# A hybrid decoder block on one core: the branch gates as seven products of halves, kept in DRAM until the projections

## The chip, the cores and the metric

The kernel runs on one core of one Trainium2 chip. The metric is the device time of one execution in microseconds; of several runs the median is given. PE is TensorE's matmul stream, PEld its weight loads, DVE is VectorE, ACT ScalarE, POOL GpSimd, SP the engine whose queue issues most DMAs.

## What is computed

One layer (D_MODEL 1024, SEQ 1024, all float32): an input projection whose columns feed four causal mixers and four gates, the gated sum of the mixers' outputs, an output projection, and a squared-ReLU MLP. The part around the change:

```python
h = rms_norm(x, norm_mix_g[l]) * (1.0 + sc1) + sh1
p = h @ w_in[l]
y_a = rwkv7_mixer(p[..., :OFF_B], ...)          # ends in ... @ rwkv_out
y_b = spatial_gating_mixer(p[..., OFF_B:OFF_C], ...)   # ... @ sg_out
y_c = short_conv_mixer(p[..., OFF_C:OFF_D], ...)       # ... @ conv_out
y_d = s5_mixer(p[..., OFF_D:OFF_G], ...)        # h = gelu(y) @ glu_w; h[:1024] * sigmoid(h[1024:])
gates = jax.nn.sigmoid(p[..., OFF_G:]).reshape(bsz, seq, N_BRANCH, D_MODEL)
merged = (gates[:, :, 0] * y_a + gates[:, :, 1] * y_b
          + gates[:, :, 2] * y_c + gates[:, :, 3] * y_d)
x = x + gt1 * (merged @ w_o[l])
```

## The kernel before, in words

Every matmul of float32 operands is three matmuls of a rounded and a remainder part: an operand is split into `hi` (ScalarE, a cast, L72) and `lo` (VectorE, the source minus `hi`, L73), and `mm3` (L110) issues hi·hi, hi·lo and lo·hi into one PSUM bank. The normed input stands in SBUF as `hh[k]`, `hl[k]`: 8 tiles of 128 features by 1024 tokens. Weights come block by block through a queue of loads (`weight_queue`, L1699; `take`, L101): a DMA on SP's queue into `raw`, then the split into `whi`, `wlo`, two buffers each.

A gate block is 128 of the 4 × 1024 gate columns. `h_mm` (L777) computes it for one half of the tokens with 8 × 3 matmuls of 128x512. `gates` (L1200) goes branch by branch (3, 1, 2 and, last, 0), block by block, half by half: gate product, sigmoid on ScalarE (L1222), the branch's own projection (6 matmuls, 12 for branch 3, whose output is a GLU), the product of the two on VectorE (L1236) and the sum over branches on POOL (L1239) or, for branch 0, on VectorE (L1241). A branch's mixer output waits in DRAM (`MX`).

Beside this runs a background: `step` (L119), called after each `mm3` (a beat), advances generators whose `yield n` asks to be called n beats later. In the stretch of the gates the background is the RWKV mixer: `rwkv_1` (L927, eight units; four feature rows are mixed, decayed and stored), `rwkv_2` (the inverse of triangular 32x32 blocks, 31 steps of a multiplication, L1051, and a sum, L1053, on VectorE) and `rwkv_3` (eight units of small matmuls, a chain in time). `mods` (L289) sums 64 slices of a weight matrix on VectorE (`macc`, L310 and L312) for later modulation vectors. Branch 0 needs the RWKV mixer, so its gates come last. Then `w_o` (L1252) and the MLP follow; the MLP's two products already use seven products of halves in place of eight.

A scheduler orders the instructions of each engine when the program is built; each engine then runs its list in order.

Of the kernel before, what the change touches and what calls it, by code (L numbers as in the profile page):

```python
# [16 lines left out]
P = 128  # L17
# [23 lines left out]
class Kern:  # L41
# [247 lines left out]
    def mods(self, M):  # L289
# [16 lines left out]
        acc = M.tile([P, HALF], F32, tag="acc", name="macc")  # L306
        for i, (sec, hf, kt) in enumerate(parts):
            w = ws[i]
            if kt == 0:
                v.tensor_scalar(acc, w, self.cact[:, 0:1], None, op0=ALU.mult)  # L310
            else:
                v.scalar_tensor_tensor(acc, w, self.cact[:, kt : kt + 1], acc, op0=ALU.mult, op1=ALU.add)  # L312
# [3 lines left out]
            if kt < KT - 1:  # L316
                continue
            pt = self.ps()
            if sec in (3, 4):
                for j in range(4):  # L320
                    self.mm(pt[:, j : j + 1], acc[:, j * P : j * P + P], self.ones)
                c = slice(4 * hf, 4 * hf + 4)
                dst = (self.sh2, self.s2)[sec - 3]
                v.tensor_tensor(dst[:, c], pt[:, :4], self.cols("ada_b")[:, sec * 8 + 4 * hf : sec * 8 + 4 * hf + 4], op=ALU.add)
                if sec == 4:
                    v.scalar_tensor_tensor(self.s2[:, c], self.s2[:, c], 1.0, self.cols("nfg")[:, c], op0=ALU.add, op1=ALU.mult)
            else:
# [872 lines left out]
    def gates(self, br, first, last):  # L1200
# [4 lines left out]
        if not first:  # L1205
            self.flush()
# [697 lines left out]
```

## Time and profile before

| | us |
|---|---|
| median of 3 runs (lowest, highest) | 1683.56 (1683.49, 1686.27) |
| the profiled execution's own time | 1685.38 |
| its span, first to last instruction | 1683.6 |
| PE busy, share of the span | 1612.0, 96% |
| mean granted TensorE clock | 0.991 |

The span is the time between the first and the last instruction; what lies around it is 1.8 us. Busy times are unions, so pipelined instructions of one engine that overlap are counted once. The stages follow each other in the span: to 353 us the norm, the first columns and the convolution; 353 to 824 the gates and projections of branches 3, 1, 2; 824 to 934 those of branch 0; 934 to 1056 the output projection and the second norm; then the MLP.

### The profile page before, as it was taken

The numbers are of one execution on the slowest core, as the hardware profiler recorded it, in microseconds if no ns is written. First come the engines' busy times: TensorE is split into PE (matmuls) and PEld (weight loads), VectorE is DVE, ScalarE is ACT, GpSimd is POOL, SyncE is SP. The second block draws the span as 40 slices with busy tenths as digits, with TensorE's granted clock in tenths as the row PEclk, the third lists the DMA queues.
The fourth block names the chain that finished last, engine by engine and source line by source line (L and its number), as shares of the span: only waits on it lengthen the run. The fifth ranks groups of instructions, "written<-read, shape, count | busy, mean of one in ns | idle before, by whom it ended". The sixth has DMA issues, their size and how long they took to land.

```text
span 1683.6 us, 22649 instructions
## 1 busy us (share of the span) xinstructions
PE 1612.0 (96%) x8083; PEld 1292.1 (77%) x8083; DVE 998.7 (59%) x1749; ACT 651.2 (39%) x1206; POOL 600.4 (36%) x485
## 2 busy tenths in 40 slices
PE   3999999999999999999999999999999999999996
PEld 2798778777777777777788877688888878888875
DVE  5673545766638824332433476965555478669986
ACT  4522134446522112212222244654554455444343
POOL 2260223112221213222101362186566465128662
PEclk9999999999999999999999999999999999999998
DMA  8423145777685245431211546364444584563332
GB/s 278 132 64 54 58 125 186 176 191 178 149 160 172 60 131 165 138 108 46 75 47 39 169 137 201 91 204 158 160 139 144 172 309 157 171 216 88 102 124 100
DMA packets 262723, 234.67 MB, mean 139 GB/s; under 512 B 79352, under 2 KB 194283, under 8 KB 262611
## 3 DMA queue, kind: packets, MB, share of 16 engines
q1 hardware_dynamic: 254002, 224.83, 44.5%
q10 hardware_dynamic: 8464, 8.01, 1.8%
q8 instruction: 64, 1.05, 0.3%
q0 software_dynamic: 144, 0.39, 0.1%
q14 instruction: 49, 0.39, 0.1%
HBM read 172.59 MB, written 60.58 MB: 138 GB/s over the span
## 4 chain that ended last, share of the span: by engine, by line
PE 36%; DVE 9%; DMA 2%; issue 2%; POOL 1%; ACT 1%; POOLq 0%; DVEq 0%; ACTq 0%; SPq 0%
PE pmm L112 21%; PE pax L112 8%; PE pch L112 7%; DVE g L73 3%; DVE xx L73 1%; DMA raw<-in_ffn_w_dram 1%; DVE m L1541 1%; DMA raw<-FA 1%; DVE n L73 1%; ACT g L72 0%; DVE wlo L73 0%; POOL ev L1531 0%; DVE m L1544 0%; DMA raw<-in_w_o_dram 0%; DVE xx L1439 0%
## 5 line engine op out<-in xcount | busy, mean ns | idle before, releaser
L112 PE MATMUL pmm<-hh,whi 128*128 128x512 f32 x704 | 285.2, 407 | 4.1 <-ACT hh L410 4.1
L112 PE MATMUL pmm<-hl,whi 128*128 128x512 f32 x704 | 278.7, 396 | 5.3 <-POOL hl L412 4.1
L112 PE MATMUL pmm<-hh,wlo 128*128 128x512 f32 x704 | 278.3, 395 | 0.0
L73 DVE TENSOR_TENSOR wlo<-raw,whi 128x512 fp32r<-128x512 f32 (+1 forms) x140 | 104.9, 786 | 130.8 <-ACT whi L72 127.6
L112 PEld LDWEIGHTS pmm<-hh,whi 128*128 128x128 f32 x704 | 132.6, 189 | 35.0 <-ACT hh L410 5.3
L112 PEld LDWEIGHTS pmm<-hl,whi 128*128 128x128 f32 x704 | 133.2, 189 | 33.7 <-POOL hl L412 4.5
L112 PEld LDWEIGHTS pmm<-hh,wlo 128*128 128x128 f32 x704 | 133.2, 189 | 29.6 <-issue 0.9
L72 ACT CAST whi<-raw 128x512 fp32r<-128x512 f32 (+1 forms) x140 | 79.0, 612 | 157.0 <-PE pmm L112 135.1
L112 PE MATMUL pmm<-g,g 128*128 128x512 f32 x456 | 107.3, 390 | 1.1 <-DVE xx L1439 1.1
L112 PE MATMUL pmm<-n,wyh 128*128 128x512 f32 x320 | 106.3, 411 | 0.8 <-ACT n L72 0.8
L73 DVE TENSOR_TENSOR g<-raw,g 128x512 fp32r<-128x512 f32 x75 | 72.0, 960 | 48.2 <-ACT g L72 48.1
L112 PEld LDWEIGHTS pmm<-g,g 128*128 128x128 f32 x456 | 85.6, 188 | 19.4 <-DVE xx L1439 1.5
L1222 ACT ACTIVATE sig<-pmm 128x512 f32<-128x512 f32 x64 | 38.2, 596 | 142.6 <-PE pmm L112 135.0
L1239 POOL TENSOR_TENSOR m<-m,sig 128x512 f32<-128x512 f32 x32 | 45.1, 1408 | 130.0 <-DVE sig L1236 129.8
L84 POOL TENSOR_TENSOR raw<-raw,gt 128x1024 f32<-128x1024 f32 x16 | 39.6, 2477 | 135.4 <-DMA raw<-in_w_o_dram 125.8
L112 PE MATMUL pmm<-g,m 128*128 128x512 f32 x256 | 81.4, 396 | 0.8 <-DVE g L73 0.6
L1236 DVE TENSOR_TENSOR sig<-pmm,sig 128x512 f32<-128x512 f32 x48 | 33.0, 686 | 69.1 <-PE pmm L112 69.0
L72 ACT CAST g<-raw 128x512 fp32r<-128x512 f32 x75 | 46.5, 620 | 69.4 <-PE pmm L112 34.5
L112 PEld LDWEIGHTS pmm<-n,wyh 128*128 128x128 f32 x320 | 60.4, 193 | 16.4 <-issue 1.2
L112 PE MATMUL pch<-g,g 128*128 128x512 f32 x222 | 59.5, 402 | 8.5 <-DVE g L73 5.7
L73 DVE TENSOR_TENSOR g<-w,g 128x512 fp32r<-128x512 f32 x65 | 64.9, 999 | 4.1 <-ACT g L72 4.1
L112 PE MATMUL pmm<-n,wyl 128*128 128x512 f32 x160 | 64.5, 403 | 0.0
(487 smaller groups left out, 3760.6 us busy)
## 6 DMA issues: line engine op xcount, KB each, us to landing
raw<-FA SPq DMA_DIRECT2D x56, 512.0 KB
raw<-in_w_in_dram SPq DMA_DIRECT2D x52, 512.0 KB
FA<-xx SPq DMA_DIRECT2D x80, 256.0 KB
raw<-in_ffn_w_dram SPq DMA_DIRECT2D x36, 512.0 KB
mod<-in_ada_w_dram SPq DMA_DIRECT2D x64, 256.0 KB
w<-in_ffn_w_dram SPq DMA_DIRECT2D x32, 512.0 KB
raw<-in_w_o_dram SPq DMA_DIRECT2D x16, 512.0 KB
FA<-ev SPq DMA_DIRECT2D x32, 256.0 KB
```

What stands on the lines that cost most here:

```text
L72: a = nc.scalar.copy(hi, src)
L73: b = (eng or nc.vector).tensor_tensor(lo, src, hi.bitcast(F32), op=ALU.subtract)
L84: nc.gpsimd.tensor_tensor(raw, raw, scale, op=ALU.mult)
L112: mm = lambda *x, **y: self.nc.tensor.matmul(*x, **y, skip_group_check=open_)
L1222: nc.scalar.activation(sg, pg, AF.Sigmoid)
L1236: v.tensor_tensor(m if first else sg, py[0], sg, op=ALU.mult)
L1239: nc.gpsimd.tensor_tensor(m, m, sg, op=ALU.add)
L1541: v.tensor_tensor(dst, x, y, op=ALU.add)
```

## The change

All gates come first. `gate_queue` and `gates` take the blocks in 16 pairs (256 gate columns), cut features, columns and tokens in halves and form each pair in seven products of 12 matmuls (Winograd's form), in an order written out by hand that weaves two pairs. The sums of halves of `h` (`h_sums`, during the convolution, and `h_blocks`) and of the weights are made on VectorE, as is one addition for three of a pair's four results; a bank accumulates products 1, 6, 7, 4 (another 5, 3) and is read in between. Weight halves are loaded on ACT's queue. The sigmoids go to a new DRAM tensor `G` (64 stores of 256 KB) and are read back (64 loads).

`merge` then does the projections: branches 3, 2, 1 woven block by block, `mx_load` having brought the mixer outputs into the tiles of `h`; then branch 0, between whose blocks the first three quarters of the output projection's first pass are placed (`next(out)`). `mods` defers a sum's matmul and its eviction by some beats (`mods_out`), and three `yield`s of `rwkv_1` grow (6 to 8, 6 to 10, 2 to 4). Cut to its core:

```diff
-                self.mm(pt[0:1], self.ones, acc)
-                yield 8
+            if kt == 2:
+                next(done, None)
+            elif kt == 4:
+                next(done, None)
+            elif kt == KT - 1:
+                done = self.mods_out(M, sec, hf, acc)
...
+    def h_sums(self):
+        for k in range(4):
+                v.tensor_tensor(f12, f(self.hh[k][:, c1]), f(self.hl[k][:, c1]), op=ALU.add)
+                v.tensor_tensor(f22, f(self.hh[k + 4][:, c1]), f(self.hl[k + 4][:, c1]), op=ALU.add)
+                v.tensor_tensor(t1, f12, f(self.hh[k][:, c0]), op=ALU.subtract)
+                v.tensor_tensor(t1, t1, f(self.hl[k][:, c0]), op=ALU.subtract)
...
+    def h_blocks(self):
+        for k in range(4):
+            self.split(self.hh[k][:, c1], self.hl[k][:, c1], self.t1[k])
+        for k in range(4):
+            v.tensor_tensor(self.f12[k], self.f22[k], self.f12[k], op=ALU.subtract)
+            v.tensor_tensor(self.f22[k], self.f22[k], self.t1[k], op=ALU.subtract)
...
+    def gate_queue(self):
+                seq += [(a, 2), (a - 1, 7)] if a > 2 else [(a - 1, 7), (a, 2)]
+                seq += [(a, 1), (a, 5), (a - 1, 4), (a, 6), (b, 2), (b, 1)]
+                seq += [(a, 7), (a, 3), (b, 5), (a, 4), (b, 6), (b, 3)]
...
+                nc.scalar.dma_start(raws[i, c], w[:, 4 * c : 4 * c + 4])
...
+            if k == 1:
+                v.tensor_tensor(A(1, 1), A(1, 1), A(2, 1), op=ALU.subtract)
+                v.tensor_tensor(A(2, 1), A(2, 1), A(2, 2), op=ALU.add)
+            elif k == 5:
+                v.tensor_tensor(A(2, 1), A(2, 2), A(1, 1), op=ALU.subtract)
+                v.tensor_tensor(A(1, 2), A(1, 2), A(2, 1), op=ALU.subtract)
...
+    def gates(self):
+        def out(i, r, c, t, src=None):
+            nc.scalar.activation(t, t if src is None else src, AF.Sigmoid)
+            self.store(self.G[br, j + r - 1, c - 1], t, 7)
+        for i, k in self.gate_seq:
+            hi, lo = self.take()
+            pt = banks[i % 2 + (2 if k in (2, 5, 3) else 0)]
+            for q in range(4):
+                self.mm3(pt, hi[:, q], lo[:, q], *B[k][q], q == 0 and k in (1, 5, 2), q == 3 and k in (4, 3, 2), open_=True)
...
+    def merge(self, todo, out=None):
+        for i, (br, j) in enumerate(todo):
+            wyh, wyl = self.take()
...
+            g_load(i + 3)
+            if (br, j) in ((0, 2), (0, 4), (0, 6)):
+                next(out)
...
+            self.conv(lambda r: r and next(sums, None))
+            self.depth = 3
+            self.h_blocks()
+            self.gates()
+            self.depth = 2
+            self.mx_load(1)
+            self.merge(self.blocks)
...
-            self.gates(0, False, True)
+            self.mx_load(0)
+            out = self.w_o()
+            self.merge([(0, j) for j in range(8)], out)
```

How the lists of the engines move, at the three places that matter below. TensorE, in the gates: before, the last two of the eight steps of a half block, and the projection behind them.

```order
L112 MATMUL pmm_3357<-hh_2_130,whi_2842 128x512
L112 MATMUL pmm_3357<-hl_2_138,whi_2842 128x512
L112 MATMUL pmm_3357<-hh_2_130,wlo_2843 128x512
L112 MATMUL pmm_3357<-hh_2_131,whi_2842 128x512
L112 MATMUL pmm_3357<-hl_2_139,whi_2842 128x512
L112 MATMUL pmm_3357<-hh_2_131,wlo_2843 128x512
L112 MATMUL pmm_3443<-n_3237,wyh_2851 128x512
L112 MATMUL pmm_3443<-n_3238,wyh_2851 128x512
L112 MATMUL pmm_3443<-n_3237,wyl_2852 128x512
```

Now, one product (`gh`, `gl`: the weight side's two parts, with the product's number 0 to 111; `m`: a made block of `h`). Four steps of three matmuls and no projection behind; a background matmul stands between.

```order
L103 MATMUL pmm_3190<-m_3129,gh_9_3432 128x512
L103 MATMUL pmm_3190<-m_3130,gh_9_3432 128x512
L103 MATMUL pmm_3190<-m_3129,gl_9_3433 128x512
L103 MATMUL pmm_3190<-m_3133,gh_9_3432 128x512
L103 MATMUL pmm_3190<-m_3134,gh_9_3432 128x512
L103 MATMUL pmm_3190<-m_3133,gl_9_3433 128x512
L133 MATMUL pax_3563<-ones,macc_3056 128x1 x4
L103 MATMUL pmm_3190<-m_3137,gh_9_3432 128x512
L103 MATMUL pmm_3190<-m_3138,gh_9_3432 128x512
L103 MATMUL pmm_3190<-m_3137,gl_9_3433 128x512
L103 MATMUL pmm_3190<-m_3141,gh_9_3432 128x512
L103 MATMUL pmm_3190<-m_3142,gh_9_3432 128x512
```

A block of 128 columns takes 48 matmuls before (two halves of 24), a pair of blocks 84 now.

VectorE, beside the triangular inverse (L1051 and L1053 before, L1056 and L1058 now): before, the remainder of a weight block (`wlo`), of a projection's weights (`wyl`) and the gate's product (L1236) stand between the steps.

```order
L73 TENSOR_TENSOR wlo_4895<-raw_4892,whi_4894 128x512 x2
L73 TENSOR_TENSOR wyl_4903<-wyr_4900,wyh_4902 128x256
L1051 TENSOR_TENSOR rpr_4497<-rti_4377,rta_4376 128x484
L1236 TENSOR_TENSOR sig_4941<-pmm_4943,sig_4941 128x512
L1053 TENSOR_REDUCE rti_4377<-rpr_4497 128x22
L312 SCALAR_TENSOR_TENSOR macc<-mod_4931,cact,macc 128x512
L1051 TENSOR_TENSOR rpr_4497<-rti_4377,rta_4376 128x529
L1236 TENSOR_TENSOR sig_4987<-pmm_4989,sig_4987 128x512
L1053 TENSOR_REDUCE rti_4377<-rpr_4497 128x23
```

Now a product's remainder (`gl`), the weight sums (L1267, L1268) and the additions from PSUM (L1308).

```order
L73 TENSOR_TENSOR gl_70_5427<-raw_5277,gh_70_5426 128x512
L1058 TENSOR_REDUCE rti_4880<-rpr_4998 128x25
L1267 TENSOR_TENSOR raw_5277<-raw_5277 128x4x128
L1308 TENSOR_TENSOR gp_5298<-pmm_3192,gp_5298 128x512
L1268 TENSOR_TENSOR raw_5277<-raw_5277,whi_5340 128x4x128
L1056 TENSOR_TENSOR rpr_4998<-rti_4880,rta_4879 128x676
L73 TENSOR_TENSOR gl_71_5448<-raw_5277,gh_71_5447 128x512
L1058 TENSOR_REDUCE rti_4880<-rpr_4998 128x26
L1270 TENSOR_TENSOR raw_5277<-whi_5340,raw_5277 128x4x128
L73 TENSOR_TENSOR gl_72_5470<-whi_5192,gh_72_5469 128x512
```

In seven products (84 matmuls) stand 14 instructions of the gates on VectorE: 7 remainders, 4 sums of weights, 3 additions. Before, a half block (30 matmuls with its projection) brought 2 or 3.

TensorE, at the end of the mixers: before, the output projection (`whi`, `wlo` against the merged `m`) follows the last gate block.

```order
L112 MATMUL pmm_8191<-hh_2_131,whi_7960 128x512
L112 MATMUL pmm_8191<-hl_2_139,whi_7960 128x512
L112 MATMUL pmm_8191<-hh_2_131,wlo_7961 128x512
L112 MATMUL pmm_8218<-n_7473,wyh_7969 128x512
L112 MATMUL pmm_8218<-n_7474,wyh_7969 128x512
L112 MATMUL pmm_8218<-n_7473,wyl_7970 128x512
L112 MATMUL pmm_8218<-n_7479,wyh_7969 128x512
L112 MATMUL pmm_8218<-n_7480,wyh_7969 128x512
L112 MATMUL pmm_8218<-n_7479,wyl_7970 128x512
L112 MATMUL pmm_8253<-whi_8056,m_7534 128x512
L112 MATMUL pmm_8253<-wlo_8057,m_7534 128x512
```

Now it begins in other banks (`pax`, `pch`) behind the first three projections of branch 0 (`mx` against `wyh`, `wyl`), with five still to come.

```order
L103 MATMUL pmm_8469<-mx_8361,wyh_8323 128x512 x2
L103 MATMUL pmm_8469<-mx_8361,wyl_8324 128x512
L103 MATMUL pmm_8482<-mx_8366,wyh_8323 128x512 x2
L103 MATMUL pmm_8482<-mx_8366,wyl_8324 128x512
L103 MATMUL pmm_8482<-mx_8371,wyh_8323 128x512 x2
L103 MATMUL pmm_8482<-mx_8371,wyl_8324 128x512
L103 MATMUL pax_8500<-whi_8389,m_8404 128x512
L103 MATMUL pax_8500<-wlo_8390,m_8404 128x512
L103 MATMUL pax_8500<-whi_8389,g_1273_8405 128x512
L103 MATMUL pax_8501<-whi_8389,m_8404 128x512
```

What stood between two projections, 24 matmuls of a gate, stands there no more.

## Rows read from the trace of the kernel before

**Rows 1.** Busy time of the whole execution, engine by engine, from the first part of the page (us, share of the span, instructions).

```profile
PE 1612.0 (96%) x8083; PEld 1292.1 (77%) x8083; DVE 998.7 (59%) x1749; ACT 651.2 (39%) x1206; POOL 600.4 (36%) x485
```

**Rows 2.** Busy time by stretch: the columns are the stretch and its length, then PE, PEld, DVE, ACT and POOL busy (us, and instructions started), the granted TensorE clock, the DMA share and GB/s. The five stretches are: gates beside the first RWKV stage; gates beside the triangular inverse (second stage); gates beside the third stage; the last branch's gates; the output projection.

```profile
353.00:471.00 118.00, 112.14 (x546) 87.38 (x545) 71.83 (x135) 69.97 (x117) 26.44 (x28) 0.97 0.70 170
514.80:580.40 65.60, 61.67 (x257) 48.29 (x256) 64.57 (x106) 14.94 (x29) 10.99 (x7) 0.97 0.45 137
621.00:810.00 189.00, 187.66 (x1563) 137.70 (x1560) 69.09 (x218) 40.93 (x100) 50.53 (x58) 1.00 0.35 103
825.00:934.00 109.00, 109.00 (x477) 89.18 (x476) 44.31 (x69) 29.05 (x54) 8.36 (x4) 1.00 0.18 55
934.00:1056.00 122.00, 116.14 (x524) 92.45 (x523) 78.82 (x122) 49.75 (x99) 52.60 (x31) 1.00 0.54 167
```

**Rows 3.** Who PE waited for between 340 and 600 us (us in total, times, longest us).

```profile
PE pax L142 <- DVE macc L312: 3.9, 2, 2.9
PE pch L142 <- DVE rar L981: 2.1, 2, 1.2
PE pch L142 <- DVE rt L937: 1.7, 1, 1.7
PE pch L142 <- DVE rbk L982: 1.0, 2, 0.9
PE pch L142 <- DVE ram L997: 0.8, 2, 0.6
PE pmm L112 <- ACT n L72: 0.8, 1, 0.8
```

**Rows 4.** Busy time by slices of 42 us, columns as in Rows 2: the three slices of the gates whose granted clock is under 1.00, and the slice with the most DMA traffic.

```profile
336.00:378.00 42.00, 38.14 (x190) 29.77 (x189) 29.39 (x60) 20.28 (x38) 6.63 (x7) 0.96 0.75 193
420.00:462.00 42.00, 40.54 (x186) 31.25 (x185) 24.76 (x47) 23.06 (x42) 9.10 (x11) 0.96 0.64 150
504.00:546.00 42.00, 39.10 (x162) 30.89 (x161) 33.72 (x74) 11.13 (x21) 5.46 (x4) 0.96 0.55 167
1344.00:1386.00 42.00, 40.29 (x173) 31.86 (x171) 28.55 (x30) 18.36 (x34) 25.77 (x17) 1.00 0.81 303
```

**Rows 5.** The same view for the instructions of L112 alone on PE (the wide matmuls), beside the first and the third RWKV stage.

```profile
353.00:471.00 118.00, 86.42 (x336) 0.97 0.70 170
621.00:810.00 189.00, 141.80 (x537) 1.00 0.35 103
```

**Rows 6.** Groups of instructions on DVE, shapes kept apart: line, engine, operation, out<-in, shape, count | busy us, mean ns of one | idle before, and what ended it.

```profile
L73 DVE TENSOR_TENSOR wlo<-raw,whi 128x512 fp32r<-128x512 f32 x132 | 99.8, 794 | 129.8 <-ACT whi L72 126.5 <-PE pmm L112 3.1
L73 DVE TENSOR_TENSOR xx<-w,xx 128x512 fp32r<-128x512 f32 x31 | 35.3, 1140 | 0.0
L1236 DVE TENSOR_TENSOR sig<-pmm,sig 128x512 f32<-128x512 f32 x48 | 33.0, 686 | 69.1 <-PE pmm L112 69.0
L73 DVE TENSOR_TENSOR wyl<-wyr,wyh 128x256 fp32r<-128x256 f32 x24 | 10.0, 415 | 0.1
L73 DVE TENSOR_TENSOR wyl<-wyr,wyh 128x512 fp32r<-128x512 f32 x8 | 5.5, 687 | 3.8 <-ACT wyh L72 3.8
L73 DVE TENSOR_TENSOR g<-sig,m 128x512 fp32r<-128x512 f32 x16 | 11.1, 692 | 11.0 <-ACT m L72 11.0
```

**Rows 7.** The multiplications (L1051) and the sums (L1053) of the triangular inverse alone, busy time in their stretch, one answer after the other (us, DVE busy with the count, granted clock, DMA share, GB/s).

```profile
514.80:580.40 65.60, 25.26 (x31) 0.97 0.45 137
514.80:580.40 65.60, 15.39 (x31) 0.97 0.45 137
```

**Rows 8.** DVE instructions in order of time in the last stage, while POOL is busy (start us, us, line, operation).

```profile
1512.40 1.28 DVE L1541 TENSOR_TENSOR m<-pmm,m 128x512 f32<-128x512 f32 x2
1513.60 0.68 DVE L73 TENSOR_TENSOR g<-w,g 128x512 fp32r<-128x512 f32 x1
1514.20 0.68 DVE L73 TENSOR_TENSOR g<-raw,g 128x512 fp32r<-128x512 f32 x1
1514.80 1.78 DVE L73 TENSOR_TENSOR g<-w,g 128x512 fp32r<-128x512 f32 x1
```

**Rows 9.** DVE, the last instruction of a unit of the first RWKV stage: the first unit's and the eighth's (start us, us).

```profile
303.70 0.41 DVE L1020 TENSOR_TENSOR rt<-pch,rt 128x256 f32<-128x256 f32 x1
471.01 0.41 DVE L1020 TENSOR_TENSOR rt<-pch,rt 128x256 f32<-128x256 f32 x1
```

**Rows 10.** Groups on ACT, columns as in Rows 6.

```profile
L72 ACT CAST whi<-raw 128x512 fp32r<-128x512 f32 x132 | 75.2, 618 | 153.1 <-PE pmm L112 135.1 <-DMA s_tt<-KP 10.3 <-PE pch L112 6.8
L1222 ACT ACTIVATE sig<-pmm 128x512 f32<-128x512 f32 x64 | 38.2, 596 | 142.6 <-PE pmm L112 135.0 <-POOL m L1239 7.5
L1623 ACT COPY m<-pmm 128x512 f32<-128x512 f32 x12 | 6.9, 586 | 8.2 <-PE pmm L112 7.9
L72 ACT CAST n<-ev 128x512 fp32r<-128x512 f32 x16 | 9.6, 616 | 6.9 <-DMA ev<-MX 6.3 <-PE pmm L112 0.6
```

**Rows 11.** A DMA issue on ACT's queue, in order of time (start us, us).

```profile
809.72 0.33 ACTq L1856 DMA_DIRECT2D gt<-GT  x1
```

**Rows 12.** Groups on POOL, columns as in Rows 6.

```profile
L84 POOL TENSOR_TENSOR raw<-raw,gt 128x1024 f32<-128x1024 f32 x16 | 39.6, 2477 | 135.4 <-DMA raw<-in_w_o_dram 125.8 <-DVE wlo L73 7.6 <-ACT hh L468 2.0
```

More of the change, by code (lines that the diff above doesn't have):

```diff
@@ L305, in mods @@
         yield 8
-        acc = M.tile([P, HALF], F32, tag="acc", name="macc")
+        done = iter(())
         for i, (sec, hf, kt) in enumerate(parts):
@@ new lines, in mods, with mods_out @@
+        yield 8
+        for _ in done:
+            yield 8
+    def mods_out(self, M, sec, hf, acc):
+        nc, v = self.nc, self.nc.vector
+        pt = self.ps()
+        if sec in (3, 4):
+            for j in range(4):
+                self.mm(pt[:, j : j + 1], acc[:, j * P : j * P + P], self.ones)
+            c = slice(4 * hf, 4 * hf + 4)
+            dst = (self.sh2, self.s2)[sec - 3]
+            v.tensor_tensor(dst[:, c], pt[:, :4], self.cols("ada_b")[:, sec * 8 + 4 * hf : sec * 8 + 4 * hf + 4], op=ALU.add)
+            if sec == 4:
+                v.scalar_tensor_tensor(self.s2[:, c], self.s2[:, c], 1.0, self.cols("nfg")[:, c], op0=ALU.add, op1=ALU.mult)
+        else:
+            self.n += 1
+            b = M.tile([1, HALF], F32, tag="w", name=f"mod_{self.n}", bufs=3)
+            c0 = sec * D + hf * HALF
+            nc.sync.dma_start(b, self.a["ada_b"][0:1, c0 : c0 + HALF])
+            self.mm(pt[0:1], self.ones, acc)
+            yield
+            v.tensor_tensor(b, pt[0:1], b, op=ALU.add)
+            nc.sync.dma_start(self.GT[sec // 4][0:1, hf * HALF : hf * HALF + HALF], b)
@@ L853, in sgu, with conv @@
             yield
-    def conv(self):
+    def conv(self, between):
         nc, v = self.nc, self.nc.vector
@@ L863, in conv @@
                 pt = self.h_mm(w, hf)
+                between(r)
                 cg.append(self.g(tag="n"))
@@ L1194, in wy_load, with mx_load @@
                 nc.sync.dma_start(wy[:, :, e], wsrc[:, :, e, cc])
[L1195 to L1196 removed]
+        hi = self.W.tile([P, 2, ne, P], F32R, tag="whi", name=f"wyh_{self.n}")
+        lo = self.W.tile([P, 2, ne, P], F32R, tag="wlo", name=f"wyl_{self.n}")
         self.split(hi, lo, wy)
[L1198 to L1207 removed]
+        return hi, lo
+    def mx_load(self, br):
+        self.flush()
+        self.mx[br] = [[None] * 2 for _ in range(2)]
+        tags = [("hh" if br in (3, 1) else "hl") + str(4 * (br in (1, 0)) + k) for k in range(4)]
         for hf in range(2):
@@ L1279, in w_o @@
                             self.store(self.X1[th * 4 + t, ch], x1[t][ch])
+                    if pc < 3 and not (th or ch):
+                        yield
             yield self.norm2(x1, xn, st, th)
@@ L1863, in build @@
             self.t2, self.t3, self.t4 = [], [], []
-            for bg in self.w_o():
+            for bg in out:
                 if self.bg is not None:
```

216 lines of the change are left out of this document (139 added, 77 removed).

## The prediction

> **What bounds the kernel now.** I read the busy times first: TensorE is busy 1612.0 of 1683.6 us, VectorE 998.7, ScalarE 651.2, POOL 600.4 [rows 1]. Then the same by stretch [rows 2]: in the last branch's gates TensorE is busy for all of 109.00 us, in which 477 matmuls start, so one wide matmul is worth 0.2285 us and each one removed is time removed, as long as the other engines keep up. Third, who TensorE waits for in the gates: VectorE, 10.3 us in all, 3.9 of it for the `mods` sums [rows 3]; three slices there have a granted clock of 0.96 [rows 4], which is half speed (1.2 of 2.4 GHz) for 0.04 x 42 / 0.5 = 3.4 us, or 1.7 us lost, after a wait each. So the reader should ask of the change: how many matmuls go, and which engine behind TensorE then has no room.
>
> **Matmuls removed.** The gates of 32 blocks take 32 x 48 = 1536 matmuls now, 16 pairs x 7 x 12 = 1344 after. Their shape is the same, so 192 x 0.2285 = **-43.9 us**. Projections, background and the rest issue the same matmuls as before.
>
> **Waits removed.** The `mods` sums are multiplied three slices late in place of at once: 3.9 us [rows 3] and the half-speed piece behind it [rows 4], 1.7, go: **-5.6**. The waits of the first RWKV stage (2.1 + 1.7 + 1.0 + 0.8) have longer yields now, but a fuller VectorE; I leave them as they are (bounds: 5.6 less; more is counted in the next step).
>
> **VectorE beside the first RWKV stage.** By the order of the lists, products 0 to 41 (504 matmuls, 115.2 us) go with six RWKV units. A unit takes (471.01 - 303.70) / 7 = 23.9 us before [rows 9]. The stretch of 118.00 us [rows 2] thus holds 4.9 units, and 336 wide matmuls [rows 5], 4.7 gate blocks. Less 336 x 0.2285 = 76.8 and 5.8 of waits, 35.4 us of small matmuls remain, 7.2 a unit. So TensorE needs 115.2 + 6 x 7.2 = 158 us. VectorE is busy 71.83 there; a gate block of branch 3 has 2 x 0.794 + 0.687 + 2 x 0.686 = 3.65 of it [rows 6], 17.0 in all, which leaves 54.8 of background, 67 for six units. A pair adds 7 remainders, 4 sums and 3 additions; two 128x512 operations on end take 1.28 us [rows 8], so 14 x 0.64 = 9.0, and 54 for six pairs. The blocks of `h` add 16 sums and differences behind the convolution and 16 remainders (the first 16 sums lie in the convolution): 32 x 0.64 = 20.5. In all 141 of 158 us: VectorE stays behind TensorE, at 90% in place of 61%. ScalarE: 69.97 less 4.7 x (3 x 0.618 + 4 x 0.596) [rows 2, 10] is 50, 61 for six units; a pair adds 7 x 0.618 + 3 x 0.586 + 4 x 0.596 and two loads at 0.33 [rows 10, 11], 9.1; 116 of 158. It too has room, but its loads stand in its list and wait until VectorE is done with the old half. At 90% with bursts at the start I take **+6** of new waits. Bounds: nothing, since the load fits; and 20, if each unit waits 3 us more, thrice what it waits now.
>
> **VectorE beside the inverse.** Its 31 steps take 25.26 + 15.39 = 40.7 us of VectorE [rows 7] and stand, by the lists, between the remainders of products 60 to 79: 20 x 12 x 0.2285 = 54.8 us of TensorE, with 20/7 x 9.0 = 25.7 for the products. 66.4 against 54.8: here VectorE is late by 11.6 us. Remainders are made three products ahead (depth 3), 8.2 us. So 3.4 us reach TensorE, with a half-speed piece of 1.7: **+5**. Bounds: 0 (now VectorE is busy 64.57 of 65.60 there [rows 2] and TensorE waits for the `mods` sums alone) and 13 (no lead).
>
> **From gates to projections.** The tiles into which `G` is read back are read by the last pair's product 7 till its end, so the first reads land only behind it; two groups of 6 matmuls and a product of 12 stand between. Waits for `MX`, read the same way, took 6.3 us in four changes of branch [rows 10]. **+3**, bounds 0 and 6. 64 stores and 64 loads of 256 KB on SP's queue, and the loads of weights on ACT's, I cost at nothing: the stores move 6.3 MB in 158 us, 40 GB/s on top of 170, and the kernel moves 303 GB/s elsewhere at a share of 0.81 [rows 2, 4]. If this cover went, loads of weights would come late; that is in the bounds above.
>
> **Projections of branches 3, 2, 1.** 384 matmuls, 87.7 us, with 128 of the third stage's 208 beats. That stage's small matmuls are now 189.00 - 537 x 0.2285 = 66 us [rows 2, 5], so 41 lie here: 128 us. VectorE: 8 x (0.687 + 2 x 0.415 + 6 x 0.686 + 2 x 0.69) = 56, and of the third stage 0.615 x (69.09 - 9 x 3.4) = 24 [rows 2, 6]; 80 of 128. **+2** for waits on the way, bounds 0 and 8. The last RWKV matmul stands 13 groups of 6, 17.8 us, ahead of branch 0, which covers the last store and load of its mixer output; if that cover went, some 8 us.
>
> **Branch 0.** 96 matmuls and 72 of the output projection, 38.4 us; VectorE 8 x (0.415 + 2 x (0.686 + 0.69 + 0.692)) + 6 x 0.794 = 41.2 [rows 6], and POOL scales each quarter of `w_o` in 2.477 [rows 12]. So VectorE is 3 us over where 24 matmuls of a gate covered it before, less what four PSUM banks hold, and the first `w_o` piece comes with less time ahead: **+5**, bounds 0 and 12 (twice the 122.00 - 116.14 that the output projection leaves idle now [rows 2]). The MLP is untouched.
>
> **Sum**, against the profiled execution: 1685.4 - 43.9 - 5.6 + 6 + 5 + 3 + 2 + 5 = 1656.9. The profiled execution lies 1.8 us above the median 1683.56, so **1655 us**. With all bounds low, 1628; with all high, 1695.
>
> **Rivals.** (1) Everything hides: the lead of three products and the longer yields take every new wait and the old ones of the first stage too. For it: VectorE is never over 90% but beside the inverse. Against it: lists run in order and ScalarE's loads tie it to VectorE. It gives 1628 to 1640.
>
> (2) VectorE becomes the bound of the gates, because its operations take longer than on a quiet POOL. The row: two remainders start 0.60 apart, and the third takes 1.78 in place of 0.68 while POOL works [rows 8]; the mean of such a group in the last stage is 1.140 [rows 6]. In the first stretch 6 x 14 + 32 = 116 operations of 128x512 come to the 67 us of background; TensorE's 158 are reached at (158 - 67) / 116 = 0.78 us an operation. From there on each 0.1 us costs 11.6 us. At 1.140, 199 us against 158, +41, where I took +6; beside the inverse 20/7 x 14 = 40 operations: 40.7 + 40 x 1.14 = 86 against 54.8, less the lead of 8.2, +23 for my 5. Together 1655 + 35 + 18 = 1708; the kernel is **slower** than before once these two places cost 28 us over my sum, which by the same working is past a mean of about 0.98. Against it: POOL is busy 26.44 of 118 us there, part of it with the sums over branches, which leave this stretch. The Trainium skill (SBUF — State Buffer, SBUF: two separate sides) says that VectorE and GpSimd share one pair of ports by an exclusive lock, held for a whole instruction, against operations with two SBUF inputs. By that rule the remainders and sums, not the additions from PSUM, would be the ones to wait, and the 1.78 agrees.
>
> (3) Half of that: some operations meet POOL or a late load, at means of 0.88 to 0.96 by the working of (2), and 13 to 25 us of the 28.5 are lost again: 1668 to 1680.
>
> (4) The removed matmuls come back as waits to the microsecond, no change: it needs 43.9 + 5.6 = 49.5 us of new ones, 28.5 more than my 21, from several places at once.
>
> (5) The change does not do what it says: a product might be longer than 12 matmuls, or gates be computed twice. The lists show 112 products of 12, so no chance is given.
>
> **How the numbers follow.** Forecast (1640 to 1668) 0.56, (1) 0.15, (3) 0.11, no change 0.06, slower 0.12: (2), alone or with a late RWKV chain. A measurement of this kernel tells about 0.2%, 3.4 us, from no change. Faster is the first three, 0.82. The range from 1631 to 1681 leaves out some 0.03 below and 0.16 above.
>
> **What would show it.** PE should start some 192 wide matmuls fewer, with its busy time down about 40 us; VectorE's should rise by 130 to 160 us, with waits of PE on the remainders (L73) beside the inverse of some 3 us in all. The wait on `macc` should be gone, and ScalarE's waits on VectorE appear at its loads (L1253). The forecast is wrong if PE waits over 25 us in the stretch of the products, if remainders there take over 0.78 us in the mean, or if PE stands still between the last RWKV matmul and branch 0.

## The result, and the profile after

| | before | after |
|---|---|---|
| median, us (4 runs each, same chip) | 1684.18 (1683.49 to 1686.27) | 1664.18 (1663.38 to 1666.47) |
| ratio, 95% interval | | 0.9872 (0.9858 to 0.9885) |
| profiled span, us | 1683.6 | 1662.4 |
| mean granted clock | 0.991 | 0.988 |

The changed kernel is 20.0 us faster. The prediction was 1655 us with a range of 1631 to 1681; the sign was right and the measured time lies inside the range. Of the 28.5 us that the sum promised, 8.5 did not come. Busy times of the changed kernel, as in [rows 1]:

```profile
PE 1579.4 (95%) x7891; PEld 1256.7 (76%) x7891; DVE 1136.6 (68%) x1973; ACT 713.3 (43%) x1316; POOL 582.1 (35%) x469
```

PE starts 192 matmuls fewer, as counted, but its busy time fell by 32.6 us, not by 43.9, and its idle time rose from 71.6 to 83.0. Two things kept PE busy for longer. The gates' matmuls start at a slower pitch (every 0.2325 us in place of 0.2285), which is 5.4 us over 1344 of them. And PE ran longer at the lower of its two clocks (1.2 GHz, granted clock 0.50): by the mean granted clock that costs (1 - 0.991) x 1683.6 = 15 us before and (1 - 0.988) x 1662.4 = 20 us now. VectorE's busy time rose by 137.9, in the forecast span of 130 to 160.

To see where, both traces are cut at the same events: the start of the third RWKV stage, the last transposition of its output, the last transposition of the second norm. Columns as in [rows 2]. First the kernel before: gates beside the first RWKV stage, beside the inverse, beside the third stage, the last gates, the output projection, the MLP. Then the changed one: products beside the first stage, products beside the inverse, the last products, the projections, branch 0 and the output projection, the MLP.

```profile
353.00:514.80 161.80, 155.94 (x736) 122.27 (x735) 85.58 (x155) 79.64 (x134) 35.34 (x35) 0.98 0.69 157
514.80:621.00 106.20, 102.27 (x450) 81.34 (x450) 76.08 (x122) 21.20 (x41) 20.32 (x15) 0.98 0.50 142
621.00:806.00 185.00, 183.66 (x1546) 134.62 (x1542) 67.80 (x216) 38.45 (x94) 49.06 (x56) 1.00 0.36 106
806.00:934.00 128.00, 128.00 (x559) 104.60 (x559) 50.94 (x82) 36.40 (x68) 13.17 (x8) 1.00 0.21 61
934.00:1057.50 123.50, 117.64 (x531) 93.54 (x530) 80.32 (x124) 51.25 (x101) 52.60 (x31) 1.00 0.53 166
1057.50:1683.00 625.50, 605.55 (x2606) 490.64 (x2605) 432.09 (x549) 295.97 (x529) 337.93 (x226) 0.99 0.47 157
```

```profile
347.00:500.00 153.00, 149.87 (x734) 116.66 (x732) 126.72 (x238) 102.74 (x180) 19.03 (x23) 0.99 0.77 205
500.00:671.00 171.00, 160.89 (x683) 124.94 (x684) 117.78 (x186) 62.20 (x109) 2.89 (x4) 0.99 0.47 128
671.00:757.00 86.00, 84.96 (x758) 61.12 (x755) 46.05 (x127) 31.31 (x66) 12.79 (x18) 0.99 0.66 207
757.00:860.00 103.00, 100.48 (x793) 73.87 (x792) 63.30 (x154) 26.18 (x62) 47.21 (x44) 1.00 0.67 207
860.00:1036.50 176.50, 163.25 (x703) 128.49 (x703) 134.26 (x202) 70.84 (x139) 70.75 (x43) 0.97 0.56 174
1036.50:1662.00 625.50, 604.85 (x2606) 489.88 (x2605) 431.54 (x549) 295.99 (x529) 337.72 (x226) 0.99 0.47 157
```

The MLP takes 625.50 us in both, so all of the change lies ahead of it. PE's idle time, length less busy, falls beside the first RWKV stage from 5.86 to 3.13, but rises beside the inverse from 3.93 to 10.11 and at the end, from the last unit's output to the second norm, from 5.86 (806 to 1057.5) to 13.25. At the end the granted clock falls too, from 1.00 to 0.97, which is (1 - 0.97) x 176.5 = 5.3 us: PE drops to the lower clock three times, at 860, 925 and 959 us, each time at the end of a wait (1.93, 1.71 and 2.17 us). I counted the wide matmuls of each stretch from PE's records and took 0.2285 us for each that it gained or lost:

| stretch | before | after | wide matmuls | lost, us |
|---|---|---|---|---|
| from 300 us to the third RWKV stage | 321.0 | 371.3 | 1111, 1290 | 50.3 - 40.9 = 9.4 |
| third stage to its last output | 185.3 | 189.0 | 521, 520 | 3.7 + 0.2 = 3.9 |
| to the last transposition of the norm | 251.2 | 176.3 | 1025, 640 | 88.0 - 74.9 = 13.1 |

That is 26.4 us lost, less 3.4 for 15 wide matmuls that already start ahead of 300 us. Against the 43.9 this gives 20.9 of the 21.2 us by which the span is shorter. The sum had 15.4 lost in place of 23.0. The first row joins the first stage, where PE waits less than before, with the inverse. In the last row, 7.4 us of more idle time and 5.3 of lower clock make up nearly all of the 13.1.

Whom PE waits for in the products (340 to 760 us: total, times, longest; the four largest):

```profile
PE pmm L103 <- ACT gp L1297: 3.2, 2, 2.2
PE pmm L103 <- DVE ev L1308: 3.1, 2, 2.2
PE pax L133 <- DVE rt L912: 2.8, 1, 2.8
PE pax L133 <- DVE macc L304: 1.8, 1, 1.8
```

The first two rows show what was not in the sum. It is not the remainders (L73) that are late, but the readings of PSUM banks: L1297 copies a product out of its bank, and L1308 adds a bank to a tile.

### The profile page after: what moved, and what is told of

The parts are those of the page before. It is cut to its first block, busy times and chain, and to the rows that moved or that the text cites. A ratio compares the mean times of both kernels' runs of the same rounds, so it can differ in the third digit from the quotient of the medians.

```text
span 1662.4 us, 22897 instructions
## 1 busy us (share of the span) xinstructions
PE 1579.4 (95%) x7891; PEld 1256.7 (76%) x7891; DVE 1136.6 (68%) x1973; ACT 713.3 (43%) x1316; POOL 582.1 (35%) x469
## 5 line engine op out<-in xcount | busy, mean ns | idle before, releaser
L103 PE MATMUL pmm<-hh,gh 128*128 128x512 f32 x256 | 105.7, 413 | 4.1 <-ACT gp L1297 3.2
L73 DVE TENSOR_TENSOR g<-raw,g 128x512 fp32r<-128x512 f32 x75 | 71.6, 955 | 49.2 <-ACT g L72 43.2
L103 PE MATMUL pmm<-mx,wyh 128*128 128x512 f32 x320 | 104.6, 407 | 0.0
L103 PE MATMUL pmm<-hh,gl 128*128 128x512 f32 x256 | 103.1, 403 | 0.1
L103 PE MATMUL pmm<-hl,gh 128*128 128x512 f32 x256 | 102.0, 399 | 0.0
L73 DVE TENSOR_TENSOR wlo<-raw,whi 128x512 fp32r<-128x512 f32 (+1 forms) x76 | 56.7, 780 | 65.7 <-ACT whi L72 65.7
L103 PE MATMUL pmm<-m,gh 128*128 128x512 f32 x256 | 83.4, 406 | 4.2 <-DVE ev L1308 3.1
L103 PE MATMUL pmm<-hh,whi 128*128 128x512 f32 x192 | 79.2, 419 | 3.5 <-ACT hh L412 3.5
L103 PE MATMUL pmm<-hl,whi 128*128 128x512 f32 x192 | 76.7, 400 | 4.5 <-POOL hl L414 3.4
L103 PE MATMUL pmm<-hh,wlo 128*128 128x512 f32 x192 | 76.2, 397 | 0.0
L72 ACT CAST g<-raw 128x512 fp32r<-128x512 f32 x75 | 46.5, 620 | 69.1 <-PE pmm L103 34.6
L72 ACT CAST whi<-raw 128x512 fp32r<-128x512 f32 (+1 forms) x76 | 42.5, 606 | 66.8 <-PE pmm L103 46.6
L103 PEld LDWEIGHTS pmm<-mx,wyh 128*128 128x128 f32 x320 | 58.3, 190 | 13.0
L73 DVE TENSOR_TENSOR g<-w,g 128x512 fp32r<-128x512 f32 x65 | 63.6, 978 | 3.8 <-ACT g L72 3.8
L73 DVE TENSOR_TENSOR gl<-raw,gh 128x512 fp32r<-128x512 f32 x64 | 44.9, 702 | 29.1 <-ACT gh L72 27.5
L72 ACT CAST gh<-raw 128x512 fp32r<-128x512 f32 x64 | 39.4, 617 | 58.7 <-PE pmm L103 51.9
L103 PE MATMUL pmm<-mx,wyl 128*128 128x512 f32 x160 | 63.4, 396 | 0.6 <-DVE wyl L73 0.6
```

What stands on the lines that cost most here:

```text
L72: a = nc.scalar.copy(hi, src)
L73: b = (eng or nc.vector).tensor_tensor(lo, src, hi.bitcast(F32), op=ALU.subtract)
L103: mm = lambda *x, **y: self.nc.tensor.matmul(*x, **y, skip_group_check=open_)
```

## The experiments

Ratios are to the kernel before, run beside it on the same chip, with 95% intervals; the changed kernel has 0.9872. Intervals are some 0.001 to 0.003 to either side (2 to 5 us), so differences between two kernels under 3 us are not read.

**Without the inverse.**

```diff
...
-            v.tensor_tensor(pv, ti[:, 0:i, 0:i]..., ta[:, 0:i, i]..., op=ALU.mult)
-            v.tensor_reduce(ti[:, i, 0:i], pv, axis=AX.X, op=ALU.add)
+            if i == 31:
+                v.tensor_tensor(ti[:, i], ti[:, i], ta[:, 0], op=ALU.mult)
             yield 2 + i // 6
```

> The changed kernel (1664.2 us median) without the multiplications and sums of the 31 inverse steps (one small multiplication stays, so the RWKV mixer's output is not the reference's): 40.7 us of VectorE go. Theory A, VectorE is what TensorE waits for in this stretch and this is all that went wrong there: the stretch of products 42 to 92 loses its 10.1 us of idle PE and most half-speed pieces, 1652. Theory B, VectorE's load costs only the two waits behind its last steps (0.66 and 2.17) and a half-speed piece of 1.9: 1659, and the waits at products 57, 58 and 92 (0.88, 0.96, 2.23) stay. Theory C, VectorE has room: 1663 to 1665.

Measured: 1654.99, ratio 0.9810 (0.9794 to 0.9825), 10 us below the changed kernel by the ratios. The same 67 us of the inverse, first in the changed kernel, then without its steps, and the whole stretch without:

```profile
555.00:622.00 67.00, 63.21 (x267) 49.86 (x268) 63.87 (x105) 23.60 (x43) 0.00 (x0) 1.00 0.31 99
```

```profile
555.00:622.00 67.00, 65.85 (x281) 52.71 (x282) 32.43 (x49) 28.50 (x50) 0.00 (x0) 1.00 0.46 125
500.00:671.00 171.00, 166.44 (x857) 129.11 (x853) 88.41 (x148) 65.93 (x118) 6.07 (x9) 1.00 0.59 162
```

VectorE's busy time halves and PE's idle time there falls from 3.79 to 1.15. The waits at 551 and 562 us stay (0.88, 0.96); the one at 668 goes. By its ratio the run lies nearest to A. But leaving the steps out also lets the third stage start 30 us sooner and takes away one of two places where the scheduler had exchanged products, so it does not show that VectorE alone is the cause.

**Weights on SP's queue.**

```diff
-                nc.scalar.dma_start(raws[i, c], w[:, 4 * c : 4 * c + 4])
+                nc.sync.dma_start(raws[i, c], w[:, 4 * c : 4 * c + 4])
```

> The changed kernel with the gate weights' halves loaded on SP's queue in place of ACT's; nothing else. In the list of PE the two places where the scheduler pulled product 58 ahead of 56 and 93 ahead of 92 are gone. Theory B, ScalarE's casts and bank reads stand behind the loads it issues, and the scheduler's order around them makes the waits 0.88, 0.96 and 2.23: 1658 to 1661. Theory A (VectorE's load): 1663 to 1665, as VectorE does the same work. Rival: SP's queue stands still for up to 8.5 us there, weights come late: 1668 or more, with PE waiting for ScalarE's casts.

Measured: 1676.19, 0.9938 (0.9926 to 0.9950): the rival came true. The products stand as written, yet PE waits for casts, and the halves that these read come late:

```profile
PE pmm L103 <- ACT gh L72: 8.3, 4, 3.4
```

How long SP's queue can stand still is seen in the changed kernel's trace too. SP's queue in order of time (start, us), and what it waited for between 534 and 546 us:

```profile
535.22 0.43 SPq L114 DMA_DIRECT2D G<-ev  x1
544.17 0.24 SPq L333 DMA_DIRECT2D mod<-in_ada_b_dram  x1
544.51 0.34 SPq L114 DMA_DIRECT2D G<-gp  x1
544.94 0.38 SPq L114 DMA_DIRECT2D G<-ev  x1
545.41 0.40 SPq L114 DMA_DIRECT2D G<-gp  x1
```

```profile
SPq L333 <- DMA raw<-in_w_in_dram: 8.4, 1, 8.4
```

After the store at 535.22 the queue issues nothing for 8.5 us. The next in line is a load of a bias row for the `mods` sums (L333). By the profile it waits until a half of the weights, loaded on ACT's queue, has landed. That load (L1253) was itself issued only at 540.45, and the bias row went at 544.17. Three stores of `G` stand behind it and go at once when it has gone. So one queue can hold the other; why a load of a bias row has to wait for that landing, no run here tests. Ahead of the third stage the same happens twice more (655 to 672 us):

```profile
SPq L1080 <- DMA raw<-in_w_in_dram: 9.9, 1, 9.9
SPq L114 <- DMA whi<-in_w_in_dram: 6.9, 1, 6.9
```

There, at the second place where products were exchanged, PE pays for it. ScalarE and its queue, then PE:

```profile
665.59 0.62 ACT L72 CAST gh<-raw 128x512 fp32r<-128x512 f32 x1 [3.17 <-PE pmm L103]
666.96 0.37 ACTq L1253 DMA_DIRECT2D raw<-in_w_in_dram  x1
667.38 0.59 ACT L1297 COPY gp<-pmm 128x512 f32<-128x512 f32 x1 [1.17 <-DVE gl L73]
```

```profile
668.02 0.50 PE L103 MATMUL pmm<-hh,gh 128*128 128x512 f32 x1 [2.23 <-ACT gp L1297]
```

The copy of a bank (L1297) can run only when what its tile held before has been stored. In ScalarE's list it stands late, behind a cast that waits for PE and a load that waits for VectorE; PE needs the bank and stands still for 2.23 us. The last store of `G` ahead of it went at 658.51, so in this run it is its place in the list that holds the copy. That the scheduler put it there because of the stores is argued here; the next run tests it.

**Stores on ACT's queue.**

```diff
-            self.store(self.G[br, j + r - 1, c - 1], t, 7)
+            nc.scalar.dma_start(self.G[br, j + r - 1, c - 1], t)
```

> The changed kernel with the 64 stores of sigmoids issued on ACT's queue right behind the sigmoid, in place of SP's seven beats later. In the list of PE all 112 products then stand as written: the two places where 58 and 93 were pulled ahead are gone. Theory B, a bank is read late because the tile it is read into waits for its store, and the store stands behind blocked loads on SP's queue: the waits 0.88, 0.96 and 2.23 and a half-speed piece go, 5 us, ratio 0.984. Theory A', all of the stretch's loss is VectorE's load of the inverse (leaving it out gave 10 us): the waits move to VectorE's remainders and the ratio stays at 0.987. Rival: 64 x 0.33 = 21 us of issues on ScalarE delay its casts: 0.990.

Measured: 1656.86, 0.9817 (0.9797 to 0.9836), 9 us below the changed kernel. That is more than B's 5: the products stand as written, the three waits are gone, and PE is idle 2.70 us in the stretch from 500 to 671 where it was 10.11, with the same inverse.

```profile
555.00:622.00 67.00, 64.30 (x276) 51.42 (x275) 62.13 (x88) 26.47 (x48) 0.00 (x0) 1.00 0.37 107
500.00:671.00 171.00, 168.30 (x795) 132.72 (x795) 120.18 (x195) 66.57 (x118) 3.18 (x5) 1.00 0.49 140
```

So the place of the stores is shown as a cause, worth about as much as the inverse was in the first experiment. The run changes two things, the queue and the moment (right behind the sigmoid in place of seven beats later), and does not say which of them counts. The two causes cannot add up, since the stretch has only about 10 us of idle time to give; no run leaves out both. What stays are two waits, 1.33 and 1.37, while VectorE is busy 62.13 of 67 us.

**Without the scaling of the output projection's weights.**

```diff
...
+        if self.wo <= 4:
+            return self.wload(w[:, 2 * pc : 2 * pc + 2])
         return self.wload(w[:, 2 * pc : 2 * pc + 2], scale=...)
```

> The changed kernel without POOL's scaling of the first four pieces of the output projection's weights by gt1 (that quarter of the projection is then unscaled). Theory L, POOL's scaling holds VectorE's operations with two SBUF inputs: six of them take 2.0 to 2.9 us in the last branch in place of 0.42 or 0.69, 11 us of VectorE, and TensorE waits there: 1656 to 1658, and no such operation over 0.9 us between the last RWKV matmul and the end of branch 0. Theory V, VectorE simply has more to do than TensorE there: 1662 to 1664, its operations as short as before but PE's waits the same.

Measured: 1659.56, 0.9841 (0.9826 to 0.9857), 5 us below the changed kernel: theory L, though its times of 1656 to 1658 were a little low. In the changed kernel, POOL and VectorE in order of time:

```profile
918.51 5.70 POOL L84 TENSOR_TENSOR raw<-raw,gt 128x1024 f32<-128x1024 f32 x2 [6.41 <-DVE n L1381]
```

```profile
917.12 0.68 DVE L1385 TENSOR_TENSOR n<-m,n 128x512 f32<-128x512 f32 x1
917.72 0.68 DVE L1381 TENSOR_TENSOR n<-pmm,n 128x512 f32<-128x512 f32 x1
918.48 0.69 DVE L73 TENSOR_TENSOR g<-n,m 128x512 fp32r<-128x512 f32 x1
919.09 2.90 DVE L1385 TENSOR_TENSOR n<-m,n 128x512 f32<-128x512 f32 x1
```

The addition of two SBUF tiles that meets POOL's scaling takes 2.90 in place of 0.68; the product with a PSUM bank (L1381) does not change. By groups, from 880 to 932 us, in the changed kernel and then without the four scalings:

```profile
L1385 DVE TENSOR_TENSOR n<-m,n 128x512 f32<-128x512 f32 x16 | 17.2, 1077 | 0.1
...
L1381 DVE TENSOR_TENSOR n<-pmm,n 128x512 f32<-128x512 f32 x16 | 10.7, 681 | 0.0
...
L73 DVE TENSOR_TENSOR wyl<-wyr,wyh 128x256 fp32r<-128x256 f32 x7 | 5.5, 780 | 0.2 <-ACT wyh L72 0.2
```

```profile
L1381 DVE TENSOR_TENSOR n<-pmm,n 128x512 f32<-128x512 f32 x20 | 13.3, 682 | 0.4 <-PE pmm L103 0.4
L1385 DVE TENSOR_TENSOR n<-m,n 128x512 f32<-128x512 f32 x16 | 12.8, 804 | 0.1
```

The additions fall from 1077 to 804 ns (the fifth scaling still meets one), the operations that read PSUM stay at 681 and 682. (1077 - 689) x 16, 689 being the mean of the same addition in the kernel before (L1241), is 6.2 us of VectorE, and the 128x256 remainders add (780 - 415) x 7 = 2.6 [rows 6]. For the stretch of branch 0 and the output projection the run without the four scalings takes 168.5 us (867.5 to 1036) at a granted clock of 1.00, where the changed kernel takes 176.5 at 0.97: with the waits the drops to the lower clock go as well. The Trainium skill (SBUF — State Buffer, SBUF: two separate sides) describes a port pair that VectorE's operations with two SBUF inputs and POOL's operations that read SBUF lock against each other; the trace agrees with it, and the operations with one input in PSUM stay as short as they were.

**The scaling on the output.**

```diff
...
+                            if not (th or ch):
+                                po = self.ev()
+                                v.tensor_tensor(po, pts[t], self.gt1[:, cc], op=ALU.mult)
+                            v.tensor_tensor(x1[t][ch], po, x1[t][ch], op=ALU.add)
```

> The changed kernel with the first four pieces of the output projection's weights unscaled and its four output tiles multiplied by gt1 when they are read (four more 128x512 operations on VectorE, 2.8 us, of which the last one or two lie on the path). The result is the reference's. Leaving the scaling out gave 5 us; theory L keeps 3 to 5 of it: ratio 0.984 to 0.985. Theory V (VectorE has too much to do there): no gain or a loss, 0.987 to 0.989.

Measured: 1657.97, 0.9837 (0.9810 to 0.9864), as theory L expected. The additions take about as long as without the scaling:

```profile
L1385 DVE TENSOR_TENSOR n<-m,n 128x512 f32<-128x512 f32 x16 | 12.6, 793 | 0.1
```

**Plain products in the new structure.**

```diff
-            if k == 1:
-                v.tensor_tensor(A(1, 1), A(1, 1), A(2, 1), op=ALU.subtract)
...
+        seq = [(i, r, c) for i in range(n) for r in (1, 2) for c in (1, 2)]
...
+            for t in range(2):
+                pt = banks[2 * (r - 1) + t]
+                rhs = of_h(4 * (c - 1), (h0, h1)[t])
```

> The changed kernel with eight plain products in place of the seven: no sums of halves of h or of the weights, each weight half is split once and used for both halves of the tokens, 1536 gate matmuls. All else (order of stages, G in DRAM, mods, yields) as changed. If the structure costs nothing and the products are worth their 192 matmuls less the waits and the pitch that they bring (43.9 less 12 to 17): 1691 to 1696. If the losses belong to the structure: 1704 to 1708, 43.9 and little else above the changed kernel. The pitch of gate matmuls, 0.2325 now against 0.2285 before: if it stays, it comes with the weights' tiles; if it falls to 0.2285, with the made blocks or the products' form.

Measured: 1690.27, 1.0018 (1.0009 to 1.0028). Just under the first case: the products with all that they bring are worth 0.0146 x 1684 = 24.6 us of their 43.9, and the structure without them costs 3. Its stretch to the third stage, and that of branch 0 and the output projection:

```profile
500.00:646.00 146.00, 146.00 (x637) 116.34 (x635) 64.13 (x99) 29.60 (x51) 2.78 (x4) 1.00 0.47 126
845.00:1065.00 220.00, 204.27 (x896) 162.12 (x896) 162.78 (x246) 80.80 (x159) 91.38 (x59) 0.99 0.58 178
```

PE has no idle time beside the inverse, but 15.73 at the end. Counted as in the table above, the last stretch loses 12.5 us (219.6 us with 832 wide matmuls), about as much as in the changed kernel. So the loss at the end belongs to the new order of stages, that beside the inverse to the products with their sums, additions and readings of banks. The gates' matmuls start every 0.2324 us here too, so the slower pitch is not the products'.

**Only the deferred sums, in the kernel before.** The diff is that of `mods` and `mods_out` above.

> The kernel before with only the deferred matmul and eviction of the mods sums, as in the change. The prediction: 3.9 us of waits and a half-speed piece of 1.7 go, ratio 0.9967. Rival: the sums are late because their loads are, and in the changed kernel one wait on macc of 1.78 stayed: half, 0.998 to 0.999.

Measured: 1682.28, 0.9979 (0.9967 to 0.9990), 3.5 us below the kernel before. Of the two waits on `macc` (3.9 us, [rows 3]) the longer stays, and a new one comes, for a remainder:

```profile
PE pax L142 <- DVE macc L313: 2.7, 1, 2.7
...
PE pmm L112 <- DVE n L73: 1.2, 1, 1.2
```

The slice from 504 to 546 us, behind the longer wait, has a granted clock of 0.96 as before. What went is the drop in the slice from 420 to 462 us (0.96 before [rows 4], 1.00 here), where PE does not wait for `macc`. So the size fits, but the waits that the prediction took off are not where the trace has the gain.

**The yields of before.**

```diff
-        yield 8
+        yield 6
...
-        yield 10
+        yield 6
...
-        yield 4
+        yield 2
```

> The changed kernel with the three yields of the first RWKV stage as before (6, 6, 2 in place of 8, 10, 4). In the list of PE the products are then issued in a much more mixed order. The prediction took 6 us of new waits beside the first stage and the trace shows none. Theory Y, the longer yields are the cover: without them waits on VectorE and ScalarE return there, 6 us or more, ratio 0.990 or above. Theory R, VectorE has room at any yield: 0.986 to 0.988.

Measured: 1669.22, 0.9898 (0.9873 to 0.9923). That is 4 us more than the changed kernel, just short of Y, but a difference of 0.0026 is not clear of the two intervals (that of the changed kernel is 0.9858 to 0.9885), so the time does not decide. The largest waits (340 to 760 us):

```profile
PE pax L133 <- DVE macc L304: 3.2, 2, 2.5
PE pmm L103 <- DVE gl L73: 2.8, 1, 2.8
PE pax L133 <- DMA rde<-DE: 2.7, 1, 2.7
```

The one of 2.8 lies beside the first stage, at 367 us, the others after 500 us, and the order of the products has changed with the yields. So whether the longer yields are the cover of the first stage stays open.

**Both repairs**, stores on ACT's queue and gt1 on the output; the diffs are those above.

> Both repairs together: the stores of the sigmoids on ACT's queue (ratio 0.9817 alone) and gt1 applied to the output of the first quarter (0.9837 alone). They lie in different stretches, so by the theory that there are two independent losses they add up: 0.9868 - 0.0051 - 0.0031 = 0.9786. If the output projection only gives back what the gates gained (a common bound behind both): 0.981 to 0.983.

Measured: 1649.07, 0.9782 (0.9765 to 0.9800). The gains of the two, 0.0055 and 0.0035 below 0.9872, add up to within the intervals, as two independent losses would.

**The inverse paced.**

This comes on top of both repairs; `gls` holds the products' remainders.

```diff
...
+            with self.tc.issue_after(self.gls[-1]):
                 v.tensor_tensor(pv, ...)
                 v.tensor_reduce(ti[:, i, 0:i], pv, axis=AX.X, op=ALU.add)
```

> As both repairs together, and in addition each of the 31 inverse steps is held back until VectorE is done with the newest product's remainder, so that the late, long steps stand one in some 1.5 products up to product 81 (now to 76) and the third RWKV stage starts some 14 us later. Theory A'' (what is left of the loss there, waits of 1.33 and 1.37 and half-speed pieces, is VectorE's packed load): 3 to 5 us less, 0.976. Rival (the RWKV chain then ends too late for the last branch, whose cover was 17.8 us): 0.979 to 0.984, with a wait of PE ahead of the last branch's projections.

Measured: 1642.56, 0.9743 (0.9722 to 0.9763), the fastest of all: 0.0039 or 6.6 us under both repairs, 22 us under the changed kernel.

```profile
555.00:622.00 67.00, 67.00 (x289) 54.15 (x288) 60.61 (x87) 26.88 (x47) 0.00 (x0) 1.00 0.32 103
500.00:671.00 171.00, 171.00 (x743) 136.41 (x742) 122.76 (x196) 69.35 (x121) 2.78 (x4) 1.00 0.47 133
```

PE is busy in all 171 us at full clock. VectorE has the same steps and products, and in the first 67 us hardly less to do (60.61, with the stores on ACT's queue alone 62.13). But the multiplications of the 31 steps now start from 545.8 to 618.2 us, where both repairs alone have them from 545.8 to 604.2. So what made PE wait there was not how much VectorE had to do, but how closely the long steps stood. Not all of the 6.6 us is shown to be that: the two waits left in this stretch were 2.7 us. The mean granted clock rose as well, from 0.990 to 0.992, and one of the drops that went lay at 352 us, ahead of the inverse.

**Split weights in another pool.**

```diff
...
-                raws[i, c] = self.W.tile([P, 4, 2 * P], F32, tag=tag, ...)
+                raws[i, c] = self.WY.tile([P, 4, 2 * P], F32, tag="y", ...)
...
-            hi, lo = (self.WY.tile([P, 4, P], F32R, tag="x", ...) for z in "hl")
+            g = self.W.tile([P, 2, 4, P], F32R, tag=("raw", "whi")[m % 2], ...)
```

> The changed kernel with two kinds of tiles exchanged: the split weights of the gates lie in the pool of the other weights, in the slots that the raw halves had, and the raw halves in theirs. The work is the same. The gates' matmuls start every 0.2325 us now, and did so with plain products too (0.2325), against 0.2285 before, where the split weights lay in that pool. If the place of the weights sets it, the pitch falls to about 0.2285 and the time by 1344 x 0.004 = 5.4 us (ratio to before 0.984 in place of 0.987). If not, pitch and time stay (0.987).

> The kernel with the paced inverse (0.9743), and the exchange of tiles of the earlier run in addition. That exchange brought the pitch of the gates' matmuls from 0.2325 to 0.2278 us, 1344 x 0.0047 = 6.3 us, and gained nothing, as PE then waited in the same stretch. Theory P, the gain was lost to those waits (VectorE and the bank reads set the pace there): with them gone it comes through, ratio 0.9705 to 0.972. Rival: the tile that holds both parts of the weights, or the raw halves' four slots, cost it elsewhere: 0.974 to 0.976.

Measured: alone 1664.98, 0.9868 (0.9849 to 0.9886), no gain; with the paced inverse 1653.37, 0.9796 (0.9771 to 0.9820), 9 us slower than the paced kernel without the exchange. The pitch did change, in the mean of some 1170 starts from 0.2325 to 0.2290 alone and to 0.2284 with the paced inverse. Matmuls started in a stretch in which PE never stands still, in the paced kernel and then with the exchange too:

```profile
622.00:664.00 42.00, 42.00 (x182) 33.91 (x181) 1.00 0.61 154
```

```profile
622.00:664.00 42.00, 42.00 (x186) 34.69 (x185) 1.00 0.59 155
```

But in the second kernel PE waits more beside the first RWKV stage: 3.43 for ScalarE at one transposition, 1.94 and 1.97 for VectorE, none of which the first has. Its profiled execution also has a mean granted clock of 0.985 against 0.992, some (1 - 0.985) x 1654.7 - (1 - 0.992) x 1640.8 = 12 us more of lower clock. So theory P has fallen, as has its rival's time: the pitch came, and waits ahead of the inverse with the drops of the clock took more than it gave. Why the exchange of tiles makes the first stage late stays open: it also joined two tiles in one and moved the scheduler's order.

## Why the prediction held, and where its sum failed

The number held in part by luck. On top of the sum came 5.4 (pitch), 2.1 (waits that stayed), 5 (inverse), about 2 (projections) and about 8 (branch 0), some 22 us. Against that, 6 + 3 were not needed (first stage, change from gates to projections), and the first stage's own waits, which the sum left as they were, shrank by some 4. The difference is about the 8.5 us by which the sum missed.

- **Matmuls removed, -43.9.** Right in count and shape. Their pitch was not: 0.2325 in place of 0.2285, 1344 x 0.004 = 5.4 us that the sum did not have.
- **Waits removed, -5.6.** It was -3.5 by the deferral alone, and by its trace not where the step "multiplied three slices late in place of at once: 3.9 us" had it. In the changed kernel the sum itself is late (VectorE waits 14.3 us for loads of `mod` from 340 to 760 us), so a wait of 1.78 stayed. Rows 3 were read too high by a little: of the "10.3 us in all" for VectorE, 0.8 is for ScalarE.
- **VectorE beside the first stage, +6.** Nothing was lost; the working (141 of 158 us) gave that, and the surcharge for bursts was not needed. VectorE is busy 126.72 of 153.00 there; over all products the remainders take 0.702 and 0.687 us in the mean. The stage's old waits shrank as well: PE's idle time went from 5.86 to 3.13, and the lower clock took (1 - 0.99) x 153.00 = 1.5 us in place of (1 - 0.98) x 161.80 = 3.2. Why is open; the run with the old yields does not decide it.
- **VectorE beside the inverse, +5.** The sum's place was right and the size short: about 10. Of the mechanism half was missing. With the stores moved, VectorE's packed steps leave PE 2.70 us idle in the place of 10.11. The rest needs the stores where the change put them, and that is the step that I set at nothing: "64 stores and 64 loads of 256 KB on SP's queue ... I cost at nothing". I weighed their bytes, and for a lost cover named late weights. What counted was when a store's turn comes and the tile that it holds till then; in the trace they stand behind DMAs that wait for weight halves on the other queue. The exchange of products stood in PE's list ahead of the run.
- **Gates to projections, +3.** PE has no wait there. **Projections, +2.** The stretch lost 3.9.
- **Branch 0, +5.** The stretch lost 13.1. I had VectorE 3 us over and added the scaling only as POOL's time (2.477 us a piece). The row that decides was in hand: rival 2 took the 1.78 [rows 8] for the gates, where POOL is hardly busy (2.89 of 171 us), and not for branch 0, where it scales. About five are shown to be that by the time of two runs (8.0 in the stretch itself without the scaling). Another term was missing whole: the drops of the clock behind the waits, 5.3 us here. Part of PE's waits for the output projection's weights (2.00, 1.00 and 1.71 for L72 and L73) goes with the scaling; what makes up the rest of the loss is not shown.
- **Rivals.** (2) was right as a mechanism and wrong in its place. The signs named for a wrong forecast did not come: PE is idle 3.13 + 10.11 + 1.04 = 14.3 us in the products, under 25, and the remainders stay under 0.78. Of the signs for a right one, the 3 us of waits on remainders beside the inverse did not come, as PE waits for bank readings there, and the wait on `macc` is not gone.
- **A slip in the bounds.** With all bounds high the working gives 1693, not 1695; the 1.8 us to the median were not taken off there.

## What to carry to other kernels

A DMA costs its bytes and also its place: ask of each store which tile it holds, who waits for that tile, and what else that queue may be waiting for when the store's turn comes, a DMA on another queue included. When work is woven into a stage in which an engine has room in the mean, look at how the scheduler packs it; pacing 31 steps came with 6.6 us without taking any work away. When two engines slow each other in one stage, go through every other stage that the change makes them share. And a wait can cost more than its own length: read the granted clock behind it.

## What was not expected of the hardware

The same matmul of 128x512 starts every 0.2325 us with its weights in one pool's tiles and every 0.2284 to 0.2290 with them in another's, without any wait. What in the place decides, no run here shows.
